# Moving low rows and low weights to the other 64 bytes of a 128-byte group

## The chip, the cores and the metric

The kernel runs on one core of one Trainium2 chip. The metric is device time in microseconds (us), the median of several runs. The inputs are float32, and the output is compared with a float32 reference.

## What is computed

Two layers (DEPTH 2) of a hybrid decoder trunk over 256 tokens of width 1024, batch 1, and a last RMSNorm. A layer normalizes, projects to 9612 columns, runs four token mixers side by side (block attention, three-branch sparse attention, stick-breaking attention, dilated attention), gates and widens each, sums them under a sigmoid and projects out:

```python
def _hybrid_layer(x, norm_w, w_in, cmp_pos, cmp_w1, cmp_w2, w_up, w_out):
    h = _rmsnorm(x, norm_w)
    proj = jnp.einsum('bsd,dc->bsc', h, w_in)
    (qa, ka, va, ga, qb, kvb, gb, nsa_g, qkvc, gc, qkvd, gd, merge) = jnp.split(...)
    ...
    widened = jnp.stack([_merge_heads(o_a) * jax.nn.silu(ga), _merge_heads(o_b) * jax.nn.silu(gb),
                         _merge_heads(o_c) * jax.nn.silu(gc), _merge_heads(o_d) * jax.nn.silu(gd)],
                        axis=2)
    u = jnp.einsum('bsiw,iwd->bsid', widened, w_up)
    merge_g = jax.nn.sigmoid(merge).reshape(b, S, N_BRANCH, D_MODEL)
    y = jnp.sum(merge_g * u, axis=2)
    return x + y @ w_out
```

## The kernel before

**Split products.** TensorE gets every large product in three parts. An operand is split into a high part, rounded to the matmul's short float32 form (`fp32r`), and a low part, the rest. A product is then high by high, high by low and low by high, three matmuls that add up in one PSUM bank. For weights, `emit_hi` (line 327) copies a loaded tile `raw` to `wh` on ScalarE and `emit_lo` (line 335) subtracts `wh` from `raw` into `wl` on VectorE. For rows, `norm_T` (line 484) makes `hh[0]` and `hl[0]` out of the normalized input; the second pair, `hh[1]` and `hl[1]`, holds the sum of the branches ahead of the output projection and, at other times, lends its halves (`blk`, lines 251 and 252) to the stacked q and k of the attention heads. `split_wid` (line 1075) splits the gated output of a mixer into `widh` and `widl`.

**The kinds of matmul.** `mm(out, a, b)` loads `a` as the stationary operand and streams `b` through it. In `mm_T` (line 593) weights are stationary and rows move; for each of 8 slices the order is (wh, hh), (wh, hl), (wl, hh). In `mm_N` (line 509) and `mm_o0` (line 579) rows are stationary and weights move: (hh, wh), (hh, wl), (hl, wh). `mm_N2` (line 521) takes the same three products in pairs, in the order in which its operands come. `mm_U` (line 1092) is the up-projection: (wh, widh), (wh, widl), (wl, widh). `mm_S` (line 860) and `mm_S2` (line 871) are the scores: a slice of q stationary, k moving from a half of `hh[1]` or `hl[1]`, then for `mm_S` the low part of k from `kl`. In the profile a matmul is written out<-moving,stationary: `pp<-hl,wh` moves `hl` through weights `wh`.

**Order.** A planner runs while the program is written: it books a time for each operation on a model of every engine (`Clock`, `Engine`, from line 134 on), by the tile's name and the part of it that is touched, and places splits, evictions and attention heads between the matmuls as they come due. Per layer come first the projections of the mixers with the attention heads between them, then, per mixer, the merge gate (`M`, an `mm_T`) and the up-projection (`U`) in turn, then the output projection (`o0` to `o3`).

**Addresses.** One pool lays all SBUF tiles one behind the other, each padded to 32 bytes, from byte 16512 of every partition on (`SB_BASE`, 129 x 128). `align` (line 222) takes 128 bytes; then follow `raw` (5 tiles), `wh` (6) and `wl` (6) of 4352 bytes (34 x 128) each, `kl` and the rest, all of whole multiples of 128 bytes up to `tm`. The 64 bytes of `skew` (line 239) stand ahead of `iden`, `xt`, `hh` and `hl` (8192 bytes a tile), `wid`, `widh`, `widl` and `qkv`.

Of the kernel before, what the change touches and what calls it, by code (L numbers as in the profile page):

```python
# [9 lines left out]
F32R = mybir.dt.float32r  # L10
# [4 lines left out]
S = 256  # L15
# [3 lines left out]
KT = D // 128  # L19
# [2 lines left out]
W_BUFS = 6  # L22
WMAX = 1072
WSLOT = 1088
SB_BASE = 16512
N_QKV = 10
N_P1 = 6

# [163 lines left out]
def kernel(ctx: ExitStack, tc: tile.TileContext, x_in, w_half, w_kvb, w_up, norm_w, pe_in,  # L192
# [14 lines left out]
    def sb(name, shape, dt=F32):  # L207
        return pool.tile(shape, dt, name=name)
# [10 lines left out]

    sb("align", [128, (-SB_BASE % 128) // 4 + 32])
    raw = Ring("raw", RAW_BUFS, [128, WSLOT])
    wh = Ring("wh", W_BUFS, [128, WSLOT], F32R)
    wl = Ring("wl", W_BUFS, [128, WSLOT], F32R)
    kl = Ring("kl", 2, [128, 4, S], F32R)
    pd = Ring("pd", 4, [128, 3 * 384])
    ptr = Ring("ptr", 6, [128, 384])
# [11 lines left out]
    iden = sb("iden", [128, 128])  # L240
    xt = sb("xt", [128, 2, D])
    hh = [sb(f"hh{i}", [128, KT, S], F32R) for i in range(2)]
    hl = [sb(f"hl{i}", [128, KT, S], F32R) for i in range(2)]
    wid = [sb(f"wid{i}", [128, 2, S]) for i in range(4)]
    widh = sb("widh", [128, 2, S], F32R)
    widl = sb("widl", [128, 2, S], F32R)
# [1238 lines left out]
```

## Time and profile before

| | us |
|---|---|
| median of 3 runs | 635.48 (634.87 to 636.95) |
| the profiled execution | 634.86 |
| its span in the trace | 632.9 |
| TensorE busy | 612.2, 5192 matmuls |
| VectorE busy | 482.1 |
| ScalarE busy | 369.5 |
| GpSimd busy | 46.3 |

The busy time of an engine is the time in which at least one of its instructions is under way. Matmuls overlap in the pipeline: one lasts some 280 ns in the record while the next starts after less than half of that. So the distance from start to start, not the duration, tells what a matmul costs in a stream. The weight load of a matmul has a row of its own (PEld).

### The profile page before, as it was taken

Reading aid. Unit: us, or ns where it says so; the run is one execution under the profiler, and the core shown is the slowest. Engines: PE = TensorE matmul, PEld = TensorE weight load, DVE = VectorE, ACT = ScalarE, POOL = GpSimd, SP = SyncE. Lnnn points to the kernel's source line nnn. Section 1 sums busy time; section 2 is a strip of 40 time slices with the busy share of each in tenths; the row PEclk is TensorE's granted clock in tenths of the full one; section 3 lists DMA queues with packets and bytes.
Section 4 is the critical chain, followed back from the end, with each engine's and each line's share of the span. In section 5 each row is a group of like instructions: output and inputs, shape, how many; then the busy total and the mean of one; then the engine's idle time right before and its main releaser. Section 6 shows DMA issues by size and latency. Waiting matters only on the chain.

```text
span 632.9 us, 12881 instructions
## 1 busy us (share of the span) xinstructions
PE 612.2 (97%) x5192; PEld 587.3 (93%) x5192; DVE 482.1 (76%) x850; ACT 369.5 (58%) x657; POOL 46.3 (7%) x59
## 2 busy tenths in 40 slices
PE   7999999999999999999999999999989999999996
PEld 6999999999998999999999899889989989999995
DVE  5887788999976665677688678899999666566673
ACT  5636744655557888445474564543575678864452
POOL 3020100111200000000001101021110000000000
PEclk9999999999999999999999999999999999999998
DMA  8942456644444345677666155645437344466811
GB/s 282 335 147 79 155 192 243 238 162 148 142 161 153 127 140 168 214 246 237 210 211 227 43 192 167 234 168 208 158 100 223 112 166 150 136 205 193 291 62 67
DMA packets 34907, 112.22 MB, mean 177 GB/s; under 512 B 4256, under 2 KB 5280, under 8 KB 34848
## 3 DMA queue, kind: packets, MB, share of 16 engines
q1 hardware_dynamic: 34560, 111.07, 52.2%
q8 instruction: 41, 0.67, 0.4%
q0 software_dynamic: 144, 0.33, 0.3%
q14 instruction: 18, 0.15, 0.1%
q10 hardware_dynamic: 144, 0.00, 0.0%
HBM read 109.61 MB, written 2.10 MB: 177 GB/s over the span
## 4 chain that ended last, share of the span: by engine, by line
PE 64%; DVE 20%; ACT 7%; issue 6%; DMA 2%; POOL 1%; SPq 0%; POOLq 0%; ACTq 0%; DVEq 0%
PE pp L151 55%; DVE wl L151 8%; DVE rope L151 4%; PE psO L151 3%; PE psT L151 3%; ACT p L151 3%; PE psS L151 3%; ACT wh L151 2%; DVE xt L151 2%; DMA raw<-w_half_dram 2%; DVE hl L151 1%; DVE p L151 1%; DVE pd L151 1%; DVE qkv L151 1%; ACT hh L151 1%
## 5 line engine op out<-in xcount | busy, mean ns | idle before, releaser
L151 PE MATMUL pp<-hh,wh 128*128 128x256 f32 x1008 | 288.2, 286 | 2.2 <-DVE xt L151 1.8
L151 PE MATMUL pp<-hh,wl 128*128 128x256 f32 x1008 | 282.1, 280 | 4.5 <-DVE wl L151 4.4
L151 PE MATMUL pp<-hl,wh 128*128 128x256 f32 x1008 | 280.9, 279 | 0.0
L151 DVE TENSOR_TENSOR wl<-raw,wh 128x1024 fp32r<-128x1024 f32 (+2 forms) x198 | 233.1, 1196 | 48.0 <-ACT wh L151 47.2
L151 ACT CAST wh<-raw 128x1024 fp32r<-128x1024 f32 (+2 forms) x198 | 189.2, 979 | 53.7 <-DMA raw<-w_half_dram 24.3
L151 PEld LDWEIGHTS pp<-hh,wh 128*128 128x128 f32 x1008 | 189.4, 188 | 9.0 <-issue 5.5
L151 PEld LDWEIGHTS pp<-hh,wl 128*128 128x128 f32 x1008 | 189.5, 188 | 6.2 <-DVE wl L151 6.1
L151 PEld LDWEIGHTS pp<-hl,wh 128*128 128x128 f32 x1008 | 189.4, 188 | 0.1
L151 PE MATMUL pp<-wh,hh 128*128 128x256 f32 (+1 forms) x320 | 84.9, 285 | 1.0 <-ACT hh L151 1.0
L151 PE MATMUL pp<-wl,hh 128*128 128x256 f32 (+1 forms) x320 | 83.1, 279 | 1.3 <-DVE wl L151 1.2
L151 PE MATMUL pp<-wh,hl 128*128 128x256 f32 (+1 forms) x320 | 83.4, 281 | 0.0
L151 PEld LDWEIGHTS pp<-wh,hh 128*128 128x128 f32 x320 | 58.3, 192 | 2.5 <-ACT hh L151 1.7
L151 PEld LDWEIGHTS pp<-wl,hh 128*128 128x128 f32 x320 | 57.3, 188 | 1.9 <-DVE wl L151 1.9
L151 PEld LDWEIGHTS pp<-wh,hl 128*128 128x128 f32 x320 | 58.0, 191 | 0.0
L151 ACT ACTIVATE p<-p,small 128x128 f32<-128x128 f32 x96 | 40.0, 449 | 27.8 <-DVE small L151 27.1
L151 DVE TENSOR_TENSOR rope<-pp,sinF 32x512 f32<-32x512 f32 x72 | 49.5, 687 | 3.3 <-PE pp L151 1.4
L151 POOL TENSOR_TENSOR xt<-xt,rope 128x512 f32<-128x512 f32 x14 | 28.0, 1998 | 168.8 <-DVE xt L151 93.2
L151 PE MATMUL pp<-widl,wh 128*128 128x256 f32 x128 | 35.9, 281 | 1.1 <-DVE widl L151 1.1
L151 PE MATMUL pp<-widh,wh 128*128 128x256 f32 x128 | 36.0, 282 | 0.0
L151 PE MATMUL pp<-widh,wl 128*128 128x256 f32 x128 | 35.8, 279 | 0.0
L151 ACT ACTIVATE tm<-pp 128x512 f32<-128x512 f32 x32 | 18.9, 591 | 22.1 <-PE pp L151 22.1
L151 ACT COPY ptr<-psT 128x384 f32<-128x384 f32 x47 | 21.4, 478 | 17.6 <-PE psT L151 17.5
(142 smaller groups left out, 666.6 us busy)
## 6 DMA issues: line engine op xcount, KB each, us to landing
raw<-w_half_dram SPq DMA_DIRECT2D x178, 512.0 KB, 4.2
raw<-w_up_dram SPq DMA_DIRECT2D x32, 256.0 KB, 3.2
raw<-w_kvb_dram SPq DMA_DIRECT2D x4, 536.0 KB, 4.5
xt<-x_in_dram SPq DMA_DIRECT2D x4, 256.0 KB, 3.5
xt<-x_in_dram SPq DMA_DIRECT2D x2, 512.0 KB, 7.1
pd<-norm_w_dram SPq DMA_DIRECT2D x2, 512.0 KB, 5.6
x_mem<-xt SPq DMA_DIRECT2D x2, 512.0 KB, 5.4
xt<-x_mem SPq DMA_DIRECT2D x2, 512.0 KB, 6.0
```

Of the source, the lines that this page charges most:

```text
L151: return f(*a, **k)
```

## The change

Only the allocation of SBUF is changed. `align` goes. Two unused tiles of 64 bytes (16 float32) are laid ahead of `wl` and ahead of `kl`, and one of 64 bytes ahead of each of the two `hl` tiles. In all 128 bytes a partition are added. No instruction is added or taken away.

```diff
--- before.py
+++ after.py
@@ -22,7 +22,6 @@
 W_BUFS = 6
 WMAX = 1072
 WSLOT = 1088
-SB_BASE = 16512
 N_QKV = 10
 N_P1 = 6
 
@@ -219,10 +218,12 @@
 
 
 
-    sb("align", [128, (-SB_BASE % 128) // 4 + 32])
+
     raw = Ring("raw", RAW_BUFS, [128, WSLOT])
     wh = Ring("wh", W_BUFS, [128, WSLOT], F32R)
+    sb("skew2", [128, 16])
     wl = Ring("wl", W_BUFS, [128, WSLOT], F32R)
+    sb("skew3", [128, 16])
     kl = Ring("kl", 2, [128, 4, S], F32R)
     pd = Ring("pd", 4, [128, 3 * 384])
     ptr = Ring("ptr", 6, [128, 384])
@@ -240,7 +241,10 @@
     iden = sb("iden", [128, 128])
     xt = sb("xt", [128, 2, D])
     hh = [sb(f"hh{i}", [128, KT, S], F32R) for i in range(2)]
-    hl = [sb(f"hl{i}", [128, KT, S], F32R) for i in range(2)]
+    hl = []
+    for i in range(2):
+        sb(f"skew{i}", [128, 16])
+        hl.append(sb(f"hl{i}", [128, KT, S], F32R))
     wid = [sb(f"wid{i}", [128, 2, S]) for i in range(4)]
     widh = sb("widh", [128, 2, S], F32R)
     widl = sb("widl", [128, 2, S], F32R)
```

## Rows read from the trace of the kernel before

**Rows 1.** The page: busy us (share) xinstructions; PEclk in 40 slices

```profile
span 632.9 us, 12881 instructions
...
PE 612.2 (97%) x5192; PEld 587.3 (93%) x5192; DVE 482.1 (76%) x850; ACT 369.5 (58%) x657; POOL 46.3 (7%) x59
...
PEclk9999999999999999999999999999999999999998
```

**Rows 2.** Busy by stretch: PE, PEld, DVE, ACT, POOL (xinstructions), PEclk, DMA, GB/s

```profile
102.00:167.00 65.00, 62.46 (x534) 59.72 (x531) 61.33 (x99) 34.30 (x53) 12.12 (x7) 1.00 0.52 174
253.00:296.00 43.00, 43.00 (x368) 42.76 (x365) 30.12 (x36) 20.91 (x29) 0.00 (x0) 1.00 0.71 234
410.00:476.00 66.00, 62.63 (x529) 59.32 (x529) 62.45 (x101) 34.15 (x53) 12.08 (x7) 1.00 0.47 162
562.00:604.00 42.00, 42.00 (x361) 41.83 (x358) 29.25 (x36) 19.91 (x28) 0.00 (x0) 1.00 0.70 238
```

**Rows 3.** Waits of TensorE: us in total, times, longest us

```profile
PE pp L151 <- DVE wl L151: 5.6, 8, 1.6
```

**Rows 4.** Groups by form: out<-moving,stationary xcount, busy us, mean ns, idle before

```profile
L151 PE MATMUL pp<-hh,wh 128*128 128x256 f32 x1008 | 288.2, 286 | 2.2 <-DVE xt L151 1.8 <-DVE qkv L151 0.3
L151 PE MATMUL pp<-wh,hh 128*128 128x256 f32 x288 | 75.7, 285 | 1.0 <-ACT hh L151 1.0
L151 PE MATMUL pp<-widh,wh 128*128 128x256 f32 x128 | 36.0, 282 | 0.0
```

**Rows 5.** Timeline, all engines: start us, us, engine, operation

```profile
254.10 0.28 PE L151 MATMUL pp<-hl,wh 128*128 128x256 f32 x1
254.10 0.19 PEld L151 LDWEIGHTS pp<-hh,wl 128*128 128x128 f32 x1
254.22 0.28 PE L151 MATMUL pp<-hh,wl 128*128 128x256 f32 x1
254.22 0.19 PEld L151 LDWEIGHTS pp<-hh,wh 128*128 128x128 f32 x1
```

**Rows 6.** Timeline of TensorE, first merge stretch

```profile
253.75 0.28 PE L151 MATMUL pp<-hl,wh 128*128 128x256 f32 x1
...
259.28 0.28 PE L151 MATMUL pp<-widh,wh 128*128 128x256 f32 x1
```

**Rows 7.** Timeline of TensorE, 24 to 35 us

```profile
24.35 0.28 PE L151 MATMUL pp<-hh,wh 128*128 128x256 f32 x1
...
35.12 0.28 PE L151 MATMUL pp<-hh,wl 128*128 128x256 f32 x1
```

**Rows 8.** Timeline of TensorE into the scores and out of them

```profile
86.09 0.28 PE L151 MATMUL pp<-hl,wh 128*128 128x256 f32 x1
...
87.00 0.28 PE L151 MATMUL psS<-hh,hl 128*128 128x256 f32 x1
...
87.48 0.28 PE L151 MATMUL pp<-hh,wh 128*128 128x256 f32 x1
...
88.07 0.28 PE L151 MATMUL pp<-hh,wl 128*128 128x256 f32 x1
```

**Rows 9.** Timeline of TensorE, up-projection into the last out-projection

```profile
603.28 0.28 PE L151 MATMUL pp<-widh,wh 128*128 128x256 f32 x1
...
604.70 0.28 PE L151 MATMUL pp<-wh,hh 128*128 128x256 f32 x1
...
608.22 0.28 PE L151 MATMUL pp<-wl,hh 128*128 128x256 f32 x1
```

**Rows 10.** Timeline of TensorE, 268 columns of weights moving

```profile
35.23 0.29 PE L151 MATMUL pp<-wh,hh 128*128 128x268 f32 x1
...
41.05 0.28 PE L151 MATMUL pp<-wh,hl 128*128 128x268 f32 x1
```

**Rows 11.** Groups by form, VectorE

```profile
L151 DVE TENSOR_TENSOR qkv<-qkv,tm 128x512 f32<-128x512 f32 x24 | 16.6, 692 | 0.8
L151 DVE TENSOR_TENSOR widl<-wid,widh 128x512 fp32r<-128x512 f32 x8 | 5.5, 685 | 0.0
```

## The prediction, made before the change was run

> **What bounds the kernel now.** The page first: TensorE is busy in 97% of the span, VectorE in 76%, and the granted clock is at its upper level of 2.4 GHz from end to end [rows 1]. The page warns that a busy TensorE is not one at its peak, so the next views ask what it waits for and how far apart its matmuls start. The stretches come in two kinds [rows 2]. In the merge stretches (253 to 296 and 562 to 604 us) TensorE has no idle time and VectorE is busy 30.1 of 43 us and 29.3 of 42. From 102 to 167 and from 410 to 476 us VectorE is busy 61.3 of 65 and 62.5 of 66 us, so there it sets the end, not TensorE. The waits confirm it: the longest wait of TensorE for anyone in the whole run is 5.6 us, for the low weights that VectorE makes [rows 3].
>
> So most of the span is a string of split matmuls: 3 x 1008 with the weights stationary and rows moving (I call them T), 3 x 288 with 256 columns of weights moving (N; 3 x 32 more have 268, K), and 3 x 128 in the up-projection (U) [rows 4]. What one costs is the distance from its start to the next start. The load of the next stationary starts within 10 ns of the present matmul [rows 5], so two reads of SBUF run side by side all the time: the moving rows of matmul n and the stationary of matmul n+1.
>
> The timeline shows this distance in two settled sizes, for the same form. In a merge stretch 47 T take 259.28 - 253.75 = 5.53 us, 117.7 ns each [rows 6]. From 24.35 us on 95 T take 10.77 us, 113.4 ns each [rows 7]. The clock is the same. I went through all starts in the timeline and put the border at 115.5 ns: T has 2190 slow and 711 fast distances, N 114 and 714, U 340 and 33; the rest are gaps at a stop. A size, once taken, holds until something interrupts the stream. One slow T costs 4.3 ns over a fast one, and 2190 x 4.3 = 9.4 us is what this change could reach in T alone.
>
> **What the change does.** No instruction is added, removed or moved; the planner's clock books tiles by name and offset, not by address, so the order stays too. Only addresses change. Before, the base is 16512 + 128 bytes, and every tile from `raw` to `tm` starts at 0 modulo 128; the 64 bytes of `skew` put all from `iden` on at 64. So W (both `wh` and `wl`) lies at 0, rows (both `hh` and `hl`) at 64. After, without the 128 bytes of `align`, `wh` stays at 0, `wl` goes to 64, and `skew3` brings `kl` back to 0. The first pair of row tiles follows: `hh[0]` at 64, `hl[0]` at 0. But the two new skews add up: `hl[1]` moves by 128 bytes and stays at 64, like `hh[1]`. The out-projection and the scores therefore get less, or other, than the title says.
>
> Now the pairs that run side by side, moving n with stationary n+1:
> - T, three in a row: before 64 with 0 each time; after (hh, wh) 64 with 0, (hl, wl) 0 with 64, (hh, wh) 64 with 0. Always opposite, but alternating.
> - N over the first row pair (dv): the mirror image, always opposite, alternating.
> - U: the second of three becomes widl at 64 with wl at 64: one in three equal. The out-projection: wl at 64 with hl[1] at 64, one in three equal. av and cv (pairs of equal products): wl with hh, and wh with hl, two in six equal.
>
> **What rows say on such pairs.** The scores are the one place where equal pairs stand now (q and k both at 64, kl at 0). A fast T stream, 8 in 0.91 us (113.8 ns), runs into them, they take 0.48 us for 4 (120 ns), and the T behind them take 118 ns (5 in 0.59 us) [rows 8]; T behind scores without a stop were slow in nearly all places. Equal pairs, then, turn the stream slow. The other way round, weights moving from 0 with rows loaded from 64 turn it fast: 12 U take 1.42 us (118.3 ns) and the N directly behind them 31 in 3.52 us (113.5 ns), without any pause between [rows 9]; every N that follows a T or U stream did so within three matmuls. N then hands the fast spacing to T (the T of [rows 7] stand directly behind an N). K is the nearest to alternation: its slices step by 1072 bytes, so the moving operand runs through all offsets. It takes 47 in 5.82 us, 123.8 ns [rows 10]; less 12 columns at 2.4 GHz (5.0 ns) that is 118.8, slow and 1.1 beyond.
>
> **The sum.** After the change one T in three is of the kind that turned the stream fast, and the other two keep fast. I take T as fast throughout, at the value of [rows 7]; the far bounds are no gain and 118.8 ns.
> - T in the VectorE-bound stretches: 436 slow ones, counted 0, since VectorE sets the end there.
> - T in the merges: 287 + 287 slow x 4.3 ns = 2.5 us, all on the path.
> - The other T: 1180 slow x 4.3 = 5.1 us; VectorE and ScalarE are late there now and then, so I take 80%, 4.1 us.
> - Out-projection, now fast (355 of 384): an equal pair in each three makes it slow, +355 x 4.3 = +1.5 us, nothing hides it. av and cv, about 190 fast now: +0.8 us. U: 33 fast now, +0.1 us.
> - VectorE: the split reads `raw` and `wh` from 0 and will write to 64. Its three operands lie mixed in the row of 692 ns and all alike in that of 685 ns [rows 11], so 7 ns per 512 columns up or down: 14 ns x some 50 splits in the VectorE-bound stretches = 0.7 us at most either way. I take 0.
>
> -2.5 - 4.1 + 1.5 + 0.8 + 0.1 = -4.2 us. The profiled execution took 634.86 us, of which the span is 632.9; the median of the three is 635.48. Profiled: 630.7; against the median 631.3. I forecast 631.0 us.
>
> The Trainium skill speaks against all of this: SBUF — State Buffer, section "SBUF: two separate sides", says that PE never waits on anyone at its SBUF ports and has a second independent read port for LDWEIGHTS. By that rule an address is worth nothing. The two spacings of one form at one clock [rows 6, 7] show a cost that this rule has no place for, though no row shows that it is the address.
>
> **The rivals.**
> 1. The spacing is set by how a stream restarts, and the address has no part in it. For it: after transposes T goes on slow or fast with nothing to tell the two apart. Against: scores and N turn it in one direction each. Time: 635.5. This is the case that the rule of the skill describes.
> 2. What counts is a matmul's moving operand against its own stationary, not the next one. Then two of three T become equal pairs (hl with wh, hh with wl), as the scores are, and nothing stays fast: 577 fast T and 545 fast N outside the VectorE-bound stretches x 4.3 ns = +4.8 us, U +0.1: 640.4. If alternation also costs what K shows, 1.1 ns more on some 3000 matmuls, 643.7. It decides wherever T directly behind an N is at 118 ns. For it: K and the scores, the only streams that change groups now, are never fast for long. Against: the load beside a matmul is the next one's [rows 5].
> 3. T keeps its present mix, since it stays opposite, and only the new equal pairs count: +1.5 + 0.8 + 0.1 = +2.4: 637.9.
> 4. T becomes fast, but VectorE takes the gain everywhere outside the merges: -2.5 + 2.4: 635.4.
>
> **Chances and range.** Forecast 0.43, rival 1 0.20, rival 2 0.22, rival 3 0.10, rival 4 0.05. A measurement of this kernel tells about 0.3% (1.9 us) from no change. So faster 0.43, same 0.25, slower 0.32. Fast end: all T and U fast, no loss at the equal pairs: -6.6 - 1.5 = -8.1, 627.4; slow end: rival 2, 640.4. I give 627 to 641; the forecast's own range is 627 to 633.5.
>
> **What would show it.** Right: T in the merges start 113 to 114 ns apart, N of the out-projection 117 to 118, the low-weight split of 1024 columns at its present time, and the same number of instructions. T at 118 behind an N shows rival 2; T in a mix of both sizes at places much like now, rival 1 or 3, told apart by the out-projection; more waits for the low weights, rival 4. The prediction is wrong if the relation of address to spacing is another than side-by-side reads.

## The result: slower by 0.84%, and the profile after

| | before | after |
|---|---|---|
| median of the runs taken together, us | 635.33 (634.87 to 636.95) | 640.13 (639.32 to 641.48) |
| difference of the two medians | | +4.80 us, 0.76% |
| ratio as estimated from the runs, 95% interval | | 1.0084 (1.0072 to 1.0095) |
| the profiled execution, us | 634.86 | 641.48 |
| its span, us | 632.9 | 639.4 |

The 0.76% between the medians lies inside the interval of the ratio. Of the runs below, two of the ten of e1_rows_only (1534 and 2108 us, far above the other eight) were slow and are left out of its median and ratio.

The forecast was 631.0 us, faster. The time lies inside the range of 627 to 641 only because that range reaches down to rival 2: it moved the other way, and lies 0.3 us from that rival's 640.4. The profiled execution is the longest of the four of after; 0.6 us of it was lost before the first long stream (its first matmul starts at 15.50 us, 14.91 in before). ScalarE waited longer there for a part of the input, and everything behind it came later. Timelines of ScalarE and TensorE, two rows of before, then two of after:

```profile
7.44 0.63 ACT L151 ACTIVATE rope<-xt 128x512 f32<-128x512 f32 x1 [1.13 <-DMA xt<-x_in_dram]
11.21 1.05 PE L151 MATMUL pp<-wh,hl 128*128 128x256 f32 x4
```

```profile
7.98 0.63 ACT L150 ACTIVATE rope<-xt 128x512 f32<-128x512 f32 x1 [2.03 <-DMA xt<-x_in_dram]
11.81 1.05 PE L150 MATMUL pp<-wh,hl 128*128 128x256 f32 x4
```

The clock is not the reason, though the page of after has 0.7 for the first fortieth and that of before 0.9 or more [rows 1]. Four matmuls of 256 columns take the same 1.05 us in both. Their starts are 213 ns apart, where later ones are 113 to 118 ns apart. For 9.2 to 15.8 us of after the granted clock is 0.50, the lower level of 1.2 GHz. So before must have been at that level too until 15.2 us, and its page does not show it.

The page of after, to be read beside [rows 1]:

```profile
span 639.4 us, 12881 instructions
...
PE 619.4 (97%) x5192; PEld 595.3 (93%) x5192; DVE 482.1 (75%) x850; ACT 369.6 (58%) x657; POOL 46.3 (7%) x59
...
PEclk7999999999999999999999999999999999999999
```

The instructions are the same, and VectorE, ScalarE and GpSimd are busy as long as they were. TensorE alone grew, by 7.2 us. Busy time by stretch of after (PE, PEld, DVE, ACT, POOL, clock, DMA, GB/s), beside [rows 2]:

```profile
102.00:167.00 65.00, 63.32 (x534) 60.41 (x532) 61.27 (x99) 35.10 (x53) 10.84 (x7) 1.00 0.50 173
414.00:480.00 66.00, 63.19 (x530) 60.15 (x529) 62.45 (x101) 34.04 (x53) 12.07 (x7) 1.00 0.47 162
567.00:609.00 42.00, 42.00 (x358) 41.76 (x355) 29.07 (x36) 19.74 (x27) 0.00 (x0) 1.00 0.71 238
```

In the two stretches that VectorE bounds TensorE does 534 and 530 matmuls, 534 and 529 in before, and is merely busy for 0.9 and 0.6 us more: there the loss falls into idle time. The same work shows it more closely. From the first T of the first of these stretches to the U behind it before takes 65.35 us (102.46 to 167.81), after 65.41 (104.48 to 169.89). In the merge stretch 358 matmuls fit where 361 did. Timeline of TensorE, before and then after:

```profile
102.46 0.39 PE L151 MATMUL pp<-hh,wh 128*128 128x256 f32 x1
...
167.81 0.28 PE L151 MATMUL pp<-widh,wh 128*128 128x256 f32 x1
```

```profile
104.48 0.38 PE L150 MATMUL pp<-hh,wh 128*128 128x256 f32 x1
...
169.89 0.28 PE L150 MATMUL pp<-widh,wh 128*128 128x256 f32 x1
```

The groups by form on VectorE (out<-in xcount, busy us, mean ns), first of before, then of after:

```profile
L151 DVE TENSOR_TENSOR wl<-raw,wh 128x1024 fp32r<-128x1024 f32 x162 | 205.2, 1281 | 41.5 <-ACT wh L151 40.7
```

```profile
L150 DVE TENSOR_TENSOR wl<-raw,wh 128x1024 fp32r<-128x1024 f32 x162 | 205.2, 1280 | 42.5 <-ACT wh L150 41.7
L150 DVE TENSOR_TENSOR qkv<-qkv,tm 128x512 f32<-128x512 f32 x24 | 16.6, 691 | 0.8
L150 DVE TENSOR_TENSOR widl<-wid,widh 128x512 fp32r<-128x512 f32 x8 | 5.5, 684 | 0.0
```

The split that now writes to the other 64 bytes takes what it took. So does all else on VectorE [rows 11]. What is left is the distance between starts of matmuls. Timeline of TensorE in after: the T behind the first long N and the K behind it, the first merge stretch, and the last out-projection.

```profile
25.48 0.28 PE L150 MATMUL pp<-hh,wh 128*128 128x256 f32 x1
...
36.73 0.28 PE L150 MATMUL pp<-hh,wl 128*128 128x256 f32 x1
36.85 0.28 PE L150 MATMUL pp<-wh,hh 128*128 128x268 f32 x1
...
42.62 0.28 PE L150 MATMUL pp<-wh,hl 128*128 128x268 f32 x1
...
256.38 0.28 PE L150 MATMUL pp<-hl,wh 128*128 128x256 f32 x1
...
261.95 0.28 PE L150 MATMUL pp<-widh,wh 128*128 128x256 f32 x1
...
608.84 0.28 PE L150 MATMUL pp<-widh,wh 128*128 128x256 f32 x1
...
610.26 0.28 PE L150 MATMUL pp<-wh,hh 128*128 128x256 f32 x1
...
613.93 0.28 PE L150 MATMUL pp<-wl,hh 128*128 128x256 f32 x1
```

| the same matmuls | before | after |
|---|---|---|
| 95 T behind a fast N | 10.77 us, 113.4 ns [rows 7] | 36.73 - 25.48 = 11.25 us, 118.4 ns |
| 47 T of the first merge | 5.53 us, 117.7 ns [rows 6] | 261.95 - 256.38 = 5.57 us, 118.5 ns |
| 31 N of the last out-projection | 3.52 us, 113.5 ns [rows 9] | 613.93 - 610.26 = 3.67 us, 118.4 ns |
| 47 K | 5.82 us, 123.8 ns [rows 10] | 42.62 - 36.85 = 5.77 us, 122.8 ns |
| 12 U | 1.42 us, 118.3 ns [rows 9] | 610.26 - 608.84 = 1.42 us, 118.3 ns |

So T did not become fast. No stream of T or N keeps 113 ns any more (the fastest 23 distances in a row are 118.0 ns in the mean for T and 117.3 for N), and those at 118 lost a little. Over all starts of the timeline (those 140 ns or more apart left out as stops) the mean distance of T went from 116.72 to 118.49 ns, of N from 114.01 to 118.13, of U from 117.45 to 118.04, of K from 123.93 to 122.68. Times their numbers: 2905 x 1.77 + 830 x 4.12 + 374 x 0.59 - 94 x 1.25 = 5.1 + 3.4 + 0.2 - 0.1 = 8.7 us of TensorE's stream, of which 4.8 us, by the medians, reach the end; in the VectorE-bound stretch above hardly any of it does (0.06 us).

### The profile page after: what moved, and what is told of

Read it like the earlier page. It is cut to its first block, busy times and chain, and to the rows that moved or that the text cites. A ratio compares the mean times of both kernels' runs of the same rounds, so it can differ in the third digit from the quotient of the medians.

```text
span 639.4 us, 12881 instructions
## 1 busy us (share of the span) xinstructions
PE 619.4 (97%) x5192; PEld 595.3 (93%) x5192; DVE 482.1 (75%) x850; ACT 369.6 (58%) x657; POOL 46.3 (7%) x59
## 4 chain that ended last, share of the span: by engine, by line
PE 68%; DVE 17%; ACT 6%; issue 5%; DMA 2%; POOL 1%; SPq 0%; POOLq 0%; ACTq 0%; DVEq 0%
PE pp L150 59%; DVE wl L150 7%; DVE rope L150 4%; PE psO L150 3%; PE psT L150 3%; PE psS L150 3%; ACT p L150 2%; ACT wh L150 2%; DMA raw<-w_half_dram 2%; DVE xt L150 1%; DVE hl L150 1%; DVE p L150 1%; ACT hh L150 1%; DVE qkv L150 1%; DVE pd L150 1%
## 5 line engine op out<-in xcount | busy, mean ns | idle before, releaser
L150 PE MATMUL pp<-wh,hl 128*128 128x256 f32 (+1 forms) x320 | 84.8, 285 | 0.0
```

Of the source, the lines that this page charges most:

```text
L150: return f(*a, **k)
```

## The experiments

"W" is `wh` and `wl`, "rows" is `hh` and `hl`; numbers are bytes modulo 128. The distance of a pair is its moving operand's address minus its stationary one's. Own pair: both operands of one matmul; side pair: the moving operand of one and the stationary of the next, which is loaded beside it. All runs carry the same 5192 matmuls but for the last three. The table has the mean distances from start to start in ns, worked out as above, and the times, each with its ratio to runs of the kernel before on the same chip. `align` (128 bytes, nothing modulo 128) is taken out in all of them but e5, where 64 bytes of it stay, and e14 to e16, where it is untouched; the diffs show it only in part.

| run | layout | T | N | U | time, us | ratio (95%) |
|---|---|---|---|---|---|---|
| before | W 0, rows 64 | 116.72 | 114.01 | 117.45 | 635.3 | 1 |
| after | + wl 64, hl[0] 0 | 118.49 | 118.13 | 118.04 | 640.13 | 1.0084 (1.0072 to 1.0095) |
| e1_rows_only, e1b | + hl[0] 0 | 117.79 | 115.72 | 115.24 | 635.84 | 1.0019 (1.0009 to 1.0029) |
| e2_weights_only | + wl 64 | 118.29 | 117.76 | 118.21 | 639.75 | 1.0077 (1.0062 to 1.0092) |
| e3_hl1_too | wl 64, both hl 0 | 118.48 | 117.79 | 118.00 | 639.96 | 1.0075 (1.0058 to 1.0092) |
| e4_one_group | all at 0 | 119.79 | 119.97 | 119.60 | 643.98 | 1.0146 (1.0131 to 1.0161) |
| e5_swapped | W 64, rows 0 | 116.73 | 114.09 | 117.35 | 634.81 | 0.9998 (0.9988 to 1.0007) |
| e6_apart32 | W 0, rows 32 | 116.98 | 118.29 | 116.84 | 636.62 | 1.0028 (1.0017 to 1.0039) |
| e7_apart96 | W 0, rows 96 | 119.84 | 117.92 | 119.88 | 643.06 | 1.0129 (1.0114 to 1.0144) |
| e8_one_slice | one of 8 slices of hl[0] at 0 | 117.52 | 114.41 | 115.74 | 635.64 | 1.0010 (1.0001 to 1.0020) |
| e9_two_slices | two of 8 slices at 0 | 117.81 | 117.16 | 117.26 | 638.55 | 1.0057 (1.0040 to 1.0074) |
| e0_none | as before, code of e8 | 116.72 | 114.01 | 117.44 | 634.95 | 1.0000 (0.9990 to 1.0009) |
| e10_wl32 | W 0 but wl 32, rows 64 | 118.54 | 118.32 | 118.72 | 640.97 | 1.0100 (1.0085 to 1.0115) |
| e11_hl32 | W 0, hh 64, hl 32 | 117.88 | 118.26 | 115.92 | 638.67 | 1.0060 (1.0045 to 1.0075) |
| e12_apart48 | W 0, rows 48 | 117.69 | 118.62 | 117.91 | 638.66 | 1.0061 (1.0044 to 1.0078) |
| e13_apart80 | W 0, rows 80 | 118.05 | 118.45 | 117.70 | 639.34 | 1.0071 (1.0056 to 1.0086) |
| e14_turn4 | before + 8 matmuls | 116.82 | 114.11 | 117.43 | 635.43 | 1.0015 (1.0006 to 1.0023) |
| e15_turn8 | before + 16 matmuls | 116.75 | 114.08 | 117.33 | 636.41 | 1.0026 (1.0016 to 1.0036) |
| e16_turn_mid | before + 8 matmuls | 115.97 | 115.93 | 115.67 | 634.65 | 0.9985 (0.9977 to 0.9994) |

**The two halves of the change.** e1 is the half with the low rows, e2 the half with the low weights.

```diff
-    sb("align", [128, (-SB_BASE % 128) // 4 + 32])
...
-    hl = [sb(f"hl{i}", [128, KT, S], F32R) for i in range(2)]
+    hl = []
+    for i, b in enumerate((64, 64)):
+        if b:
+            sb(f"skew_l{i}", [128, b // 4])
+        hl.append(sb(f"hl{i}", [128, KT, S], F32R))
```

> Half of the change: only the row tiles are moved (hl[0] to 0 modulo 128, hl[1] stays at 64), all weights stay at 0. Three theories now. Own pair: a stream of matmuls can be fast (113.4 ns) only if no matmul's moving operand lies in the group of its own stationary. Side pair: only if no moving operand lies in the group of the next matmul's stationary. Alternation: only if neither operand changes its group from one matmul to the next, equal or not. All three have T and the dv, av and cv products slow here (one in three equal, and alternating), so 117.5 to 118.5 ns, and the out-projection, whose rows are not moved, fast at 113.4 ns as before: about 638 to 639 us. If the out-projection is slow too, all three are wrong.

> The same kernel as the one with only the rows moved, once more, for its trace: that one's median was 636.1 us, 1.3 us above the kernel before, not the 638 to 639 us that was expected. Expected in the trace by the time: the out-projection fast at 113.4 ns as before, and T near 117.2 ns in the mean, half a ns above the kernel before, with fast stretches left or with three unequal distances in each slice.

```diff
-    sb("align", [128, (-SB_BASE % 128) // 4 + 32])
...
+    sb("skew2", [128, 16])
     wl = Ring("wl", W_BUFS, [128, WSLOT], F32R)
+    sb("skew3", [128, 16])
```

> The other half: only the low weights are moved to 64, all rows stay at 64. Each theory has every kind of matmul slow (T, N, U and the out-projection: one in three equal, and alternating), 117 to 119 ns: about 640 us. If the loss of the change lies with the rows alone, this is at 635.

The trace of e1 is that of e1b, the same kernel (635.77 us). The rows alone cost 0.19%, the weights alone 0.77%, nearly all of the change. In e1 the alternating T fall into a triple of 118, 115 and 120 ns. All three theories had the time at 638 to 639 us; it came out lower, and U, whose operands were not moved, turned faster (115.24 ns), which none of them has. The out-projection keeps 113.3: 30 N in 609.41 - 606.01 = 3.40 us. Its `hl[1]` lies 128 bytes farther from the weights than in before, and that changes nothing, which speaks for 128 as the number to count by. In e2 every kind of stream is at 117.8 to 118.3.

```profile
606.01 0.28 PE L150 MATMUL pp<-wh,hh 128*128 128x256 f32 x1
...
609.41 0.28 PE L150 MATMUL pp<-wh,hh 128*128 128x256 f32 x1
```

**The out-projection without an equal side pair.** After, and `hl[1]` at 0 as well, so that every side pair of the out-projection is opposite while two of its three own pairs are equal.

```diff
-    for i in range(2):
-        sb(f"skew{i}", [128, 16])
+    for i, b in enumerate((64, 0)):
+        if b:
+            sb(f"skew_l{i}", [128, b // 4])
         hl.append(sb(f"hl{i}", [128, KT, S], F32R))
+    sb("skew_w", [128, 16])
```

> The change, and hl[1] put at 0 as its title says; wid and all behind it stay where they were. In the out-projection every side pair is then opposite, two of three own pairs are equal (in the change one of three), and both operands alternate. Side pair: the out-projection is fast again (113.4 ns), 384 x 4.7 ns = 1.8 us less than the change, 638.3 us. Own pair: it is slower than in the change, above 118 ns, 640 to 642 us. Alternation: as in the change, 118 ns, 640 us.

By the side pairs the out-projection should have been fast again. It starts 31 N in 613.72 - 610.07 = 3.65 us, 117.7 ns, and the time stays at after's. So opposite side pairs are not enough for the fast spacing, and the theory of side pairs, on which the forecast stood, falls. The theory of own pairs misses too: it had the out-projection slower than in after (118.4). Rows of TensorE's timeline in e3:

```profile
610.07 0.28 PE L150 MATMUL pp<-wh,hh 128*128 128x256 f32 x1
...
613.72 0.28 PE L150 MATMUL pp<-wl,hh 128*128 128x256 f32 x1
```

**No alternation at all.** All operands in one group; and W and rows exchanged.

```diff
-    sb("skew", [128, 16])
```

> The kernel before with the 64 bytes of skew taken out: weights and rows all at 0, every own pair and every side pair equal, no alternation. Own pair and side pair: nothing can be fast, T and N at 118 ns or more, 640 us or more. Alternation: the mix of fast and slow streams as before, T 116.7 ns and N 114.0 ns in the mean, 634 to 637 us.

```diff
-    sb("align", [128, (-SB_BASE % 128) // 4 + 32])
+    sb("align", [128, 16])
```

> Weights at 64 modulo 128, rows at 0: opposite and constant as in the kernel before, but with the two places exchanged. If only the distance of the two operands counts, the mix of fast and slow streams is as before (T 116.7 ns, N 114.0 in the mean) and the time 634.7 us, within 1 us. If a moving operand at 0 is what turns a stream fast, T becomes fast (113.4) and N slow (117.7): T gains 1754 x 4.3 ns of which some 85% on the path, N loses 545 x 4.3: about 631 us.

In e4 nothing alternates, and it is the slowest layout of all: nearly every start is 120 ns from the next. The 48 T of a merge in the timeline of e4:

```profile
263.11 0.28 PE L150 MATMUL pp<-hh,wh 128*128 128x256 f32 x1
...
268.87 0.28 PE L150 MATMUL pp<-widh,wh 128*128 128x256 f32 x1
```

268.87 - 263.11 = 5.76 us, 120.0 ns. So alternation alone is not the cause either; the distance counts by itself. Whether that of the own pair or that of the side pair does, e4 cannot tell, since both are 0 throughout. e5 changes nothing, neither the time nor the places where a stream is fast or slow. It is therefore not a fixed half of the 128 bytes, but the one operand against the other.

**Other constant distances.** Only the size of `skew` differs (32 and 96 bytes instead of 64).

```diff
-    sb("skew", [128, 16])
+    sb("skew", [128, 8])
```

> Rows 32 bytes behind weights modulo 128, constant. All in one place gave 120.0 ns everywhere (644.0 us), 64 bytes apart gives a mix of 113.3 and 117.8 (634.7 us). If the cost falls steadily with the distance of the two operands, this lies between: 638 to 641 us. If what counts is only whether the two stand in the same half of 128 bytes, it is like one place, 644 us; if any distance does, 635 us or less.

> Rows 96 bytes behind weights modulo 128, constant. If distance counts without sign, as with 32 bytes. If the sign counts (the moving operand ahead of or behind the stationary), T and N part ways here and in the run with 32 bytes, in opposite senses: T faster in the one, N in the other. 634 to 644 us.

For 48 and 80 bytes the row tiles are cut out of wider ones (here 48; `hl` likewise; for 80 the cut begins at 4):

```diff
-    hh = [sb(f"hh{i}", [128, KT, S], F32R) for i in range(2)]
+    hh_pair = sb("hh", [128, 2 * KT * S + 32], F32R)[:, 28:28 + 2 * KT * S]
+    hh = [hh_pair[:, i * KT * S:(i + 1) * KT * S].rearrange("p (k t) -> p k t", k=KT) for i in range(2)]
```

> All rows of both pairs 48 bytes behind the weights, no alternation (U's rows stay at 64). T at 48 lies between 116.7 (at 64) and 117.0 (at 32): 116.9 ns expected if the spacing goes smoothly with the distance; N at 80 lies between 114.0 (at 64) and 118.3 (at 96): 116 ns. Time 635.5 to 637. If what counts is the 32-byte or 64-byte group, T and N are as with rows at 32: 117.0 and 118.3, time 636.6. If the best place lies between the four that were tried, T falls below 115 and the time below 633.

> All rows 80 bytes behind the weights, no alternation (U's rows stay at 64). T at 80 lies between 116.7 (at 64) and 119.8 (at 96): 118 ns if smooth; N at 48 between 117.9 (at 32) and 114.0 (at 64): 116 ns; time 638 to 640. If the group of 64 bytes counts, as before: 116.7, 114.0, 635.3.

At distances 0, 32, 48, 64, 80 and 96 a constant T takes 119.8, 117.0, 117.7, 116.7, 118.1 and 119.8 ns. N, whose distance has the other sign, takes at 0, 32 (e7), 48 (e13), 64, 80 (e12) and 96 (e6) 120.0, 117.9, 118.5, 114.0, 118.6 and 118.3. It does not go smoothly with the distance, the first case of the expectations for 48 and 80. Nor is the signed distance all: at 32 T and N differ by 0.94 ns, at 96 by 1.55. Of these, 64 alone has stretches that stay at 113.3 ns; with 116.7 for T it is a mix of 113.3 and 117.8. No constant distance was better than that of before.

**Alternation between good distances.** `wl`, or both `hl`, at 32. For T all own and side pairs then lie at 64 or 32, and none is equal.

```diff
+    sb("skew2", [128, 8])
     wl = Ring("wl", W_BUFS, [128, WSLOT], F32R)
+    sb("skew3", [128, 24])
```

> Low weights alternate with the high ones, but by 32 bytes: W 0, wl 32, all rows 64. Moving minus stationary is 64, 64, 32 in the three T (own pairs) and 64, 32, 64 beside the next load: only distances at which T ran in 116.7 to 117.0 ns while they were constant. In N the second of three is at 96, where a constant N took 118.3 ns. If only the distance of a pair counts: T 116.7 to 117.2 ns with stretches of 113.3, out-projection about (114 + 118 + 114) / 3 = 115.4 ns, time 635.3 to 637. If a change of group between matmuls costs by itself, whatever the distance: T 118 or above with no stretch of 113.3, N 117 to 118, time 639 to 640 as with the low weights at 64.

```diff
+    sb("skew_l", [128, 24])
     hl = [sb(f"hl{i}", [128, KT, S], F32R) for i in range(2)]
+    sb("skew_m", [128, 8])
```

> Low rows alternate with the high ones by 32 bytes: all W 0, hh 64, both hl at 32. T has own distances 64, 32, 64 and 64, 32, 64 beside the next load; N has 64, 64, 96. If only the distance of a pair counts: T 116.7 to 117.2 ns with stretches of 113.3, out-projection 115 to 116, time 635.3 to 637. If a change of group costs by itself: T at 117.8 or above in a triple and no stretch of 113.3, out-projection 117 to 118, time 637 to 640.

Timeline of e10: 48 T of a merge, and 31 N of the last out-projection.

```profile
262.18 0.28 PE L150 MATMUL pp<-hh,wh 128*128 128x256 f32 x1
...
267.89 0.28 PE L150 MATMUL pp<-widh,wh 128*128 128x256 f32 x1
...
609.59 0.28 PE L150 MATMUL pp<-wh,hh 128*128 128x256 f32 x1
...
613.26 0.28 PE L150 MATMUL pp<-wl,hh 128*128 128x256 f32 x1
```

The 31 N take 3.67 us, 118.4 ns; one in three is at 96, so they tell little. T takes 5.71 us for 48, 119.0 ns: more than the slow 117.8 at a constant 64 and the 117.0 at a constant 32. So the change from one distance to another between matmuls has a price of its own, some 1 to 2 ns and the fast spacing, and rival 2's equal own pairs are not needed for it. e11 says the same with less weight: T 117.88, in a pattern of six (118, 119, 119, 113, 120, 118 ns in a merge) that holds one short distance.

**One slice in eight, and two.** The low rows of slice 0, or of slices 0 and 4, lie at 0, the rest at 64; a kernel with the same code and no slice moved stands beside them.

```diff
+KICKS = (0,)
...
+    far = [k in KICKS for k in range(KT)]
+    lo_at = [S * k + 16 * sum(far[i] != far[i - 1] for i in range(1, k + 1)) for k in range(KT)]
...
-            mm(o, hi, hl[0][:, k, :], start=False, stop=False)
+            mm(o, hi, lo_row(k), start=False, stop=False)
```

> Weights at 0 and rows at 64 as before, but one slice of the eight of the first low row tile (k = 0) lies at 0, so one matmul in 24 of T has a moving operand in the other group; the splits that fill it take one more VectorE instruction each. With only the rows moved, T that alternates in each slice was held at 118.2, 115.6 and 119.7 ns in turn (117.8 in the mean), but U, whose operands were not moved, became fast behind it (115.2 ns in the mean, 117.4 before). If a short change of group pushes a stream into the fast spacing and a constant relation then keeps it there, T falls from 116.7 to 114 to 115 ns, U stays near 115, and with some 0.6 of the sum reaching the end the time is 630 to 632 us. If each change pushes it into the slow spacing, T rises to 117.5 and the time to 636 or 637. If one slice in eight does nothing, 634.9.

> The same with two slices of the eight (k = 0 and 4). If a change of group sets the fast spacing, more of T is in the disturbed triples than with one slice (6 matmuls in 24 plus the way back): T 115 to 116 ns, 632 to 634 us. If a change sets the slow spacing, as with one slice or a little more, 637 us.

> The control for the two: the same code with no slice moved, all low rows at 64. Addresses relative to each other are those of the kernel before, the whole pool begins 128 bytes lower. Every theory: as the kernel before, 634.9 us within 1 us, T 116.7 ns and N 114.0 ns.

The idea was that one disturbance would turn the stream fast and the rest keep it. It missed (635.64 us where 630 to 632 was hoped for, and 638.55 with two slices): of the 48 T of a merge in e8 some two dozen were irregular and the last 21 slow again. e0 shows that the code of these kernels costs nothing.

**Can the spacing be turned?** The layout of before. Ahead of the first T of each merge stretch stand four extra matmuls (eight in e15), rows stationary and weights moving, into a PSUM bank that nobody reads afterwards; their result is not used.

```diff
+    def mm_turn(h):
+        o = psS.free[0][:, 0:256]
+        for k in range(4):
+            tc.nc.tensor.matmul(o, hh[0][:, k, 0:128], his[h][:, 256 * (k % 4):256 * (k % 4) + 256],
+                                start=(k == 0), stop=(k == 3))
+
-    def mm_T(o, h):
+    def mm_T(o, h, turn=False):
+        if turn:
+            mm_turn(h)
...
+            turn = len(merges) % 16 == 11
-                yield (lambda: mm_T(bank[:, 256 * t:256 * t + 256], h0 + t),
+                yield (lambda: mm_T(bank[:, 256 * t:256 * t + 256], h0 + t, turn and t == 0),
```

> The layout of before, with four more matmuls at the head of each of the two merge stretches (rows hh stationary, 256 columns of wh moving, into a free PSUM bank of the scores that nobody reads): extra work whose result is not used. They cost 8 x 0.114 to 0.118 us = 0.9 us. If a spacing, once taken, holds until something interrupts the stream, and a stream of rows stationary and weights moving turns it fast, then the 288 T and 72 U behind them in each layer run at 113.4 instead of 117.7 ns: -3.1 us, in all -2.2 us, 633.0 to 633.5. If fast is not handed on (T goes back to 118 after some matmuls), +0.9 us: 636.

> The same with eight more matmuls a stretch, +1.8 us, for the case that four are too few to turn the stream: 634 if it turns and holds, 637 if it does not. If four already turn it, this is 0.9 us above e14_turn4.

e16 differs from e14 in one character: `t == 1`, so that the four come 24 T later, inside an unbroken stream.

> The same four extra matmuls of e14_turn4, but 24 matmuls later, so that they stand in the middle of an uninterrupted T stream instead of behind the PSUM transposes and the products of the attention weights (their result is not used, here as there). In before every N that stood directly behind a T or U stream turned fast after two or three matmuls, while those behind an interruption were slow for long. If it is the uninterrupted swap of the two operands that turns the stream, the four start slow, slow, fast, fast and the 264 T and 72 U behind them run at 113.4 ns: (336 x 4.3 - 4 x 115) x 2 = -2.0 us, 633.0. If the spacing cannot be turned from outside, +0.9 us, 635.9, as e14_turn4 did.

Timeline of e14, then of e16:

```profile
253.61 0.74 PE L596 MATMUL psS<-wh,hh 128*128 128x256 f32 x4
254.18 0.28 PE L151 MATMUL pp<-hh,wh 128*128 128x256 f32 x1
...
259.84 0.28 PE L151 MATMUL pp<-widh,wh 128*128 128x256 f32 x1
```

```profile
254.72 0.28 PE L151 MATMUL pp<-hl,wh 128*128 128x256 f32 x1
...
257.31 0.28 PE L151 MATMUL pp<-hh,wl 128*128 128x256 f32 x1
257.43 0.63 PE L596 MATMUL psS<-wh,hh 128*128 128x256 f32 x4
257.89 0.28 PE L151 MATMUL pp<-hh,wh 128*128 128x256 f32 x1
...
260.62 0.28 PE L151 MATMUL pp<-widh,wh 128*128 128x256 f32 x1
...
295.98 0.28 PE L151 MATMUL pp<-wh,hh 128*128 128x256 f32 x1
...
604.28 0.28 PE L151 MATMUL pp<-wh,hh 128*128 128x256 f32 x1
...
607.94 0.28 PE L151 MATMUL pp<-wl,hh 128*128 128x256 f32 x1
```

Here, behind an interruption, four or eight matmuls turn nothing: 48 T in 5.66 us, 117.9 ns, and the run is longer by 0.15% and 0.26%, the price of the extra work. They were slow themselves (behind the first start 114, 118 and 118 ns apart in e14) and handed that on to T, in 4 of 4 places of e14 and e15. It is not that every N behind an interruption is slow, as the expectation of e16 has it: of nine such streams of ten or more N in before seven are fast from the sixth matmul on at the latest, and two (at 111.93 and 419.33 us) stay slow. In the unbroken stream four do it: 22 T ahead of them up to 257.31 are 117.7 ns apart, 24 T behind them take 260.62 - 257.89 = 2.73 us, 113.8, and every T and U from there to 295.98 is fast. From the first T of the stretch to the first N of the out-projection it takes 41.48 us where before took 42.51, extra work included, and the same in the second layer. Then came what was not expected: the out-projection behind the now fast U starts slow and stays so, 31 N in 607.94 - 604.28 = 3.66 us, 118.1 ns, against 3.52 [rows 9]. It gives back 0.6 us in the first layer (19.86 us to the next transposes, 19.23 before) and 0.8 us in the second (29.0 us to the end of the span, 28.2 before). 1.03 x 2 - 0.6 - 0.8 = 0.7 us is left, 634.65 against 635.32 measured: the fastest of the kernels, though by less than the 0.3% that a measurement of this kernel tells from no change. Turning the stream back ahead of the out-projection was not tried.

## Why the prediction was wrong, and where it was right

**The step that failed** is the first of the sum: "After the change one T in three is of the kind that turned the stream fast, and the other two keep fast. I take T as fast throughout". It rests on the reading of [rows 9] that "weights moving from 0 with rows loaded from 64 turn it fast". Every N of before that stands directly behind T or U is indeed fast. But every such T or U was slow, so before could not tell "turns it fast" from "turns it over". In the six kernels with all pairs at a constant 64 (before, e0, e5, e14 to e16) an N directly behind a slow T or U is fast in 28 of 28 places and slow behind a fast one in 2 of 2, both in e16. T and U hand their spacing to each other in 288 of 288, and a fast N hands it to T in 18 of 18. The slow extra matmuls of e14 and e15, which are of N's kind, hand slow to T, 4 of 4. So an N was not of "the kind" that is fast. In these six kernels the change from moving rows to moving weights, in an unbroken stream, turns the spacing over, and the change back keeps it. That is why one swap and back, in e16, turns a stream. The terms that hung on this, -2.5 and -4.1 us, came out as losses: T +1.77 ns on average.

**The alternation** was the second miss. The prediction named it ("Always opposite, but alternating") and had the row for it, K at 118.8 "slow and 1.1 beyond" (K itself came out 1.25 ns lower in after), yet took it as the far bound only. In after T is at 118.4 and 118.5 ns in the two places shown, and e10 (119.0) shows that alternating costs as much even without an equal pair. After has both, two equal own pairs in three and the alternation, and no run tells their shares in it apart. The loss is 0.7 ns on the T that stood at 117.8 and 5 ns on those at 113.3.

**The side pairs** were the third: the forecast let the moving operand count against the next stationary. [rows 5] shows that the two reads run side by side, not that their conflict is what sets the spacing; e3 spoke against it, with every side pair of the out-projection opposite and its N at 117.7 ns.

**What held.** Only addresses changed: the instructions and VectorE's 1280 ns are as before. The two spacings of one form at one clock do depend on the address, 113.3 to 120.0 ns by layout, so rival 1, that the address has no part in it, is out: e4 costs 1.46% with nothing else changed. Which of the two spacings a stream at 64 takes, though, is not set by the address. The prediction put the Trainium skill, SBUF — State Buffer, section "SBUF: two separate sides", against itself with the rule that PE never waits on anyone at its SBUF ports and has a second, independent one for LDWEIGHTS. As the prediction reads that rule, both would be the same; measured, T takes 119.8 ns in e4 and 116.7 in before, the same instructions at the same clock. The out-projection became slow, as said, and its N went 5 ns up, but by luck: the reason given was the equal side pair, and e3 has it slow without one. In the first VectorE-bound stretch nothing reached the end, as the sum took it. The scores (118.1 and 118.0 ns, counted like the rest) and U barely moved. Two readings of rows were off, without weight in the sum: the clock was not at 2.4 GHz until 15.2 us, and the 5.6 us of [rows 3] are eight waits together, the longest 1.6 us.

**Rival 2** gave the time, 640.4, by its count: nothing stays fast, 577 T and 545 N at 4.3 ns. That it came so near is in part luck, since a fast T lost 5 ns, not 4.3, and of the 8.7 us that TensorE's stream lost only 4.8 reached the end. Its test was the right one: T directly behind an N is at 118.4 ns, where [rows 7] has 113.4. Its mechanism is only part of it. Equal pairs do cost (e4, all own and side pairs equal: 120.0), but the T of e10 have none and are as slow as those of after. What it held for a surcharge, the alternation, is enough alone for such a loss. Its 643.7 with both was too high: the T that were slow lost 0.7 ns, not 1.1.

**What stays open.** How much of the loss of after is due to its equal pairs and how much to the alternation, why a change of distance between matmuls costs, why 64 alone allows 113.3 ns, and what a stream takes when it starts behind an interruption. Nor is the spacing all there is to the state: in e1 and e8 a U that ends fast is followed by a fast out-projection, 4 of 4, and in e9 a slow U by a slow one, 2 of 2. U and N stand there at the same places modulo 128 as in before, and only T ahead of them alternates. So the rule of turning over holds where all pairs stand at a constant 64, and not beyond.

## What to carry to other kernels

Where streams of split matmuls bound the time, measure their distance from start to start and lay the moving and the stationary operands at one constant distance modulo 128, here 64 bytes. An operand that alternates between two places lost the fast spacing in its streams and cost 0.2% to 1.0% of the time, less than a bad constant distance (1.5% at 0, 1.3% at 96). A behaviour that always follows one event is not yet caused by it: look for a place where the state ahead of the event was the other one, and if the trace has none, an extra instruction or two make one cheaply.

## What the runs showed of the hardware

- The distance of 256-column matmuls at one granted clock of 2.4 GHz goes by the two operands' addresses modulo 128: 120.0 ns for equal ones, 113.3 or 117.8 at 64 apart, 117.0 to 119.8 on average at 32, 48, 80 and 96. Exchanging the two groups changes nothing (e5); exchanging the roles does (e7: T 119.84, N 117.92; e6: T 116.98, N 118.29).
- At 64 apart both spacings are stable over hundreds of matmuls, and four matmuls with the roles swapped, in an unbroken stream, turned 117.7 into 113.8 ns or less for the next 38 us (e16); behind an interruption they did nothing (e14, e15).
- An operand that alternates by 32 or 64 bytes from one matmul to the next keeps T off the fast spacing: 117.8 to 118.5 ns in the mean (e1, e2, e10, e11, after), against 116.7 at a constant 64.
